# Giving VectorE's order by hand in the v stage, with 64 more gathered columns, and moving a product of the gates three groups later

## The chip, the cores and the metric

The kernel runs on one core of one Trainium2 chip. The metric is the device time of one execution, in microseconds. Before the change it is 2059.61 us, the median of three runs (2057.92 to 2060.23). The engines of the core are named as in the profile: PE is TensorE (matmuls), PEld its weight loads, DVE is VectorE, ACT is ScalarE, POOL is GpSimd, SP is SyncE, which only issues DMAs here.

## What is computed

One layer of a streaming encoder for 256 tokens of 2048 columns: a convolution branch and a state-space branch, attention over 256 memory rows, then a layer of product-key experts, and a last RMS norm. Only the experts matter for the change:

```
idx, g = the 128 chosen experts of a token (8 heads x 16) and their gates
u = jnp.take(u_tab, it, axis=0)
act = jax.nn.gelu(jnp.einsum("td,tkd->tk", xt, u))
v = jnp.take(v_tab, it, axis=0)
return jnp.einsum("tk,tkd->td", gt * act, v)
```

There are 16384 experts; both tables are 16384 x 2048 in float32.

## The kernel before, in words

The 256 tokens lie in two tiles of 128 (tt = 0 and 1). The layers ahead of the experts are done by about 790 us and are not touched. The experts are computed in three stages.

**The u stage with the dense part.** Of each u row the first 768 columns are multiplied densely: `dense()` (L960) loads all 128 blocks of 128 experts, transposes them on PE (L972) and multiplies them by all tokens (L978). The other 1280 columns are gathered: `Route.dot` (L925) issues one indirect DMA of POOL per slot (L928, five buffers) and one DVE instruction that multiplies and sums (L930). There are 256 dots, counted by `tick`. The loop at L1125 writes the order of DVE out by hand (`manual_schedule`, L1122): what is emitted first runs first on DVE. `Pace` (L1076) feeds the routing and the dense part between the dots at so many steps per dot.

**Settling.** At dot number `SETTLE_AT` (L1131) the rest of the dense part is emitted, and from then on `settle()` (L1086) is paced at 2.2 steps per dot. Settling picks from the dense scores those of the chosen experts: per group of four tokens `onehots` (L992: PE, then ACT Relu), `select` (L1010: PE), `pick` (L1023: a DVE product, L1026, then PE, L1028). When all 32 groups of a tile are picked, `finish` (L909) adds the gathered part, takes the Gelu curve (L915) and multiplies by the gates (L918, DVE), and transposes the result back. Then `left` and `build` (L1031, L1047) write the coefficients of four tokens, spread over all 16384 experts, into `W[tt]`. The one-hot `L` of `left` is made either by PE and ACT (L1043, L1044) or by a DVE comparison (L1039); `route.tt and g % 2` says which. Tile 0 is picked first; its builds run among the picks of tile 1. `settle` runs `routes[0].finish()` between the two, with four steps of its own. What is left of the builds follows after the last dot, at L1157 to L1163, where the order of DVE is again the planner's.

**The v stage.** The output is the chosen v rows times their coefficients. Of the 2048 columns `DC` = 1472 are done densely: for each block b of 128 experts the loop at L1202 makes float32r high and low parts of the weights (`wh`, `wl`, L1208 on ACT and L1209 on DVE) and of the loaded rows (`split`, L102: `vh` on ACT, L103; `vl` on DVE, L104), and 18 matmuls accumulate in PSUM: two tiles, three column chunks of 512, 512 and 448, three products each (L1218 to L1220). The other `GC` = 576 columns are gathered: `gathered()` (L1178) issues one indirect DMA per slot (L1183, six buffers) and one DVE multiply-add into `accg` (L1185), 256 in all, a little over two per block. SP loads `vr` (L1211) four buffers ahead. `vh`, `vl`, `wh` and `wl` have two buffers each. In this stage a planner that simulates the engines sets the order on every engine; it may bring an instruction forward when its inputs are there. After the loop DVE adds the residual (L1228), ACT squares (L1229, L1230), and each tile is normed and stored (L1231 to L1242).

## Time and profile before

| | |
|---|---|
| median of three runs | 2059.61 us |
| the profiled execution | 2058.54 us |
| its span, first to last instruction | 2056.8 us |
| mean granted clock of PE over the span | 0.982 |
| PE busy | 1960.9 us, 95% of the span |
| DVE busy | 1681.5 us, 82% |
| ACT busy | 999.4 us, 49% |
| POOL busy | 786.2 us, 38% |
| all DMA | 571.78 MB, mean 278 GB/s |

The times of the rows are microseconds from the start of the span. Busy times of PE are modelled ends of pipelined matmuls, so neighbouring matmuls overlap in the rows; the distance between two starts is what one costs in a stream. A number in square brackets at the end of a row is the idle time of the engine just before it, and what ended it.

### The profile page before, as it was taken

Reading aid. Unit: us, or ns where it says so; the run is one execution under the profiler, and the core shown is the slowest. Engines: PE = TensorE matmul, PEld = TensorE weight load, DVE = VectorE, ACT = ScalarE, POOL = GpSimd, SP = SyncE. Lnnn points to the kernel's source line nnn. Section 1 sums busy time; section 2 is a strip of 40 time slices with the busy share of each in tenths; the row PEclk is TensorE's granted clock in tenths of the full one; section 3 lists DMA queues with packets and bytes.
Section 4 is the critical chain, followed back from the end, with each engine's and each line's share of the span. In section 5 each row is a group of like instructions: output and inputs, shape, how many; then the busy total and the mean of one; then the engine's idle time right before and its main releaser. Section 6 shows DMA issues by size and latency. Waiting matters only on the chain.

```text
span 2056.8 us, 33321 instructions
## 1 busy us (share of the span) xinstructions
PE 1960.9 (95%) x12361; PEld 1682.5 (82%) x12379; DVE 1681.5 (82%) x2757; ACT 999.4 (49%) x1586; POOL 786.2 (38%) x589
## 2 busy tenths in 40 slices
PE   7899999998999999999999999989999999999996
PEld 7888886786899888888888878867678888888885
DVE  6699999895665557999976667888869899899998
ACT  5775765454644445333333323556554444444444
POOL 1011111000000004443446655453128777677775
PEclk9999999999999999999999999999999999999998
DMA  8888788857855567999999999988539999999996
GB/s 245 198 226 222 202 220 227 229 179 221 286 174 177 168 203 266 305 312 321 322 363 403 408 390 396 302 289 266 160 143 337 359 339 336 346 339 336 342 339 226
DMA packets 203108, 571.78 MB, mean 278 GB/s; under 512 B 31410, under 2 KB 39459, under 8 KB 202818
## 3 DMA queue, kind: packets, MB, share of 16 engines
q1 hardware_dynamic: 135810, 307.48, 44.4%
q0 software_dynamic: 67136, 262.18, 38.0%
q8 instruction: 97, 1.59, 0.3%
q14 instruction: 65, 0.53, 0.1%
HBM read 556.74 MB, written 12.85 MB: 277 GB/s over the span
## 4 chain that ended last, share of the span: by engine, by line
PE 56%; DVE 15%; issue 11%; DMA 8%; POOL 7%; ACT 1%; SPq 0%; POOLq 0%; DVEq 0%; ACTq 0%
PE acc L1220 8%; PE acc L1219 8%; PE acc L1218 8%; POOL u L928 7%; DVE u L930 5%; PE mm L216 4%; PE mm L215 4%; PE mm L214 4%; PE mm L206 3%; PE mm L207 3%; PE mm L205 3%; PE pw L1054 3%; DMA w_lo<-in_w_kv_mem 3%; PE y L1019 1%; DMA xc<-in_mem 1%
## 5 line engine op out<-in xcount | busy, mean ns | idle before, releaser
L1183 POOL DMA_INDIRECT v<-in_peer_v,vidx x256 | 394.1, 1539 | 180.9 <-DVE accg L1185 70.5
L930 DVE SCALAR_TENSOR_TENSOR u<-u,hnF 128x1280 f32<-128x1280 f32 x256 | 384.5, 1505 | 81.5 <-DMA u<-in_peer_u,uidx 79.5
L928 POOL DMA_INDIRECT u<-in_peer_u,uidx x256 | 300.3, 1173 | 324.3 <-DVE u L930 235.6
L978 PE MATMUL sy<-hnT,ut 128*128 128x256 f32 x1536 | 357.5, 385 | 13.4 <-ACT ut L974 12.4
L191 ACT CAST w_hi<-w_raw 128x1024 fp32r<-128x1024 f32 (+2 forms) x228 | 231.4, 1017 | 246.1 <-PE mm L207 116.0
L978 PEld LDWEIGHTS sy<-hnT,ut 128*128 128x128 f32 x1536 | 287.2, 193 | 54.7 <-ACT ut L974 16.3
L196 DVE TENSOR_TENSOR w_lo<-w_raw,w_hi 128x1024 fp32r<-128x1024 f32 (+2 forms) x192 | 227.4, 1186 | 112.9 <-ACT w_hi L191 110.7
L103 ACT CAST vh<-vr 128x1472 fp32r<-128x1472 f32 x128 | 183.1, 1431 | 251.5 <-PE acc L1219 167.9
L1219 PE MATMUL acc<-vh,wl 128*128 128x512 f32 (+1 forms) x768 | 295.4, 385 | 0.0
L1220 PE MATMUL acc<-vl,wh 128*128 128x512 f32 (+1 forms) x768 | 293.7, 385 | 0.2 <-DVE vl L104 0.2
L216 PE MATMUL mm<-aT_hi,w_lo 128*128 128x256 f32 x960 | 270.6, 289 | 17.9 <-DMA w_lo<-in_w_in 6.8
L1218 PE MATMUL acc<-vh,wh 128*128 128x512 f32 (+1 forms) x768 | 275.9, 384 | 2.4 <-ACT vh L103 2.4
L214 PE MATMUL mm<-aT_hi,w_hi 128*128 128x256 f32 x960 | 276.2, 290 | 0.3 <-ACT w_hi L191 0.3
L215 PE MATMUL mm<-aT_lo,w_hi 128*128 128x256 f32 x960 | 273.8, 287 | 0.0
L104 DVE TENSOR_TENSOR vl<-vr,vh 128x1472 fp32r<-128x1472 f32 x128 | 216.7, 1693 | 45.5 <-ACT vh L103 34.7
L1185 DVE SCALAR_TENSOR_TENSOR accg<-v,coef,accg 128x576 f32<-128x576 f32 x256 | 208.6, 815 | 4.1
L216 PEld LDWEIGHTS mm<-aT_hi,w_lo 128*128 128x128 f32 x960 | 181.9, 193 | 24.4 <-DMA w_lo<-in_w_in 8.0
L214 PEld LDWEIGHTS mm<-aT_hi,w_hi 128*128 128x128 f32 x960 | 185.0, 193 | 5.8 <-issue 3.7
L215 PEld LDWEIGHTS mm<-aT_lo,w_hi 128*128 128x128 f32 x960 | 185.4, 193 | 3.4 <-issue 2.0
L974 ACT COPY ut<-ut 128x768 f32<-128x768 f32 x128 | 100.4, 800 | 168.0 <-PE ut L972 143.8
L1219 PEld LDWEIGHTS acc<-vh,wl 128*128 128x128 f32 x768 | 144.5, 188 | 30.6 <-DVE wl L1209 0.4
L1218 PEld LDWEIGHTS acc<-vh,wh 128*128 128x128 f32 x768 | 144.7, 188 | 28.3 <-ACT vh L103 2.6
(385 smaller groups left out, 3233.3 us busy)
## 6 DMA issues: line engine op xcount, KB each, us to landing
vr<-in_peer_v SPq DMA_DIRECT2D x128, 736.0 KB
raw<-in_peer_u SPq DMA_DIRECT2D x127, 384.0 KB
w_raw<-in_w_kv_mem SPq DMA_DIRECT2D x64, 512.0 KB
w_raw<-in_w_in SPq DMA_DIRECT2D x48, 512.0 KB
w_raw<-in_w_out SPq DMA_DIRECT2D x32, 512.0 KB
w_raw<-in_w_q_mem SPq DMA_DIRECT2D x32, 512.0 KB
w_raw<-in_w_o_mem SPq DMA_DIRECT2D x32, 512.0 KB
w_lo<-in_w_kv_mem POOLq DMA_DIRECT2D x24, 512.0 KB
```

The source lines that it names most:

```text
L191: S.copy(hi, raw)
L196: V.tensor_sub(lo, raw, hi.bitcast(F32))
L214: PE.matmul(o, wh, ah, start=first and cb % 2 == 0, stop=False, skip_group_check=True)
L215: PE.matmul(o, wh, al, start=False, stop=False, skip_group_check=True)
L216: PE.matmul(o, wl, ah, start=False, stop=last and end, skip_group_check=True)
L928: G.indirect_dma_start(out=u, out_offset=None, in_=a["peer_u"].rearrange("e (q c) -> (e q) c", c=GU), in_offset=bass.IndirectOffsetOnAxis( ...
L930: V.scalar_tensor_tensor(u, u, 1.0, hnF[:, self.tt, :], op0=ALU.mult, op1=ALU.mult, accum_out=self.act[:, j:j + 1])
L978: PE.matmul(ps[:, b % 2, :], ut[:, k, :], hnT[:, k, :], start=k == 0 and b % 2 == 0, stop=k == KD - 1 and b % 2 == 1, skip_group_check=True)
L1183: G.indirect_dma_start(out=v, out_offset=None, in_=table, in_offset=bass.IndirectOffsetOnAxis(ap=vidx[tt][:, j:j + 1], axis=0))
L1218: PE.matmul(o, wh[:, tt, :], vh[:, cs_], start=b == 0, stop=False)
L1219: PE.matmul(o, wl[:, tt, :], vh[:, cs_], start=False, stop=False)
L1220: PE.matmul(o, wh[:, tt, :], vl[:, cs_], start=False, stop=b == NB - 1)
```

## The change

- `GC` goes from 576 to 640, so `DC` from 1472 to 1408 and the third column chunk from 448 to 384.
- In the v stage the order of DVE is given by the program. Weights are split for two blocks at once (`WGROUP` = 2, tiles of 128 x 256, three buffers), one group ahead, among the gathers of every odd block. Within a block and tile the products with `vl` come after all those with `vh`. The products of tile 1 in the last two blocks come after all others. Gathers are asked for at the same pace as before.
- A Sqrt on a scratch column is emitted at block 110.
- In `settle`, `routes[0].finish()` is begun where it was, and its second half (the product with the gates, the transpose back) is emitted at group 3 of tile 1.
- `left` of tile 1 uses DVE's comparison in 21 groups of 32 where it used it in 16.
- `SETTLE_AT` goes from 176 to 179.

```diff
-GC = 576
+GC = 640
-WL_POOL = 0
+WGROUP = 2
+EARLY = 8
-SETTLE_AT = 176
+SETTLE_AT = 179
...
+    eps_j = consts.tile([P, 1], F32, name="eps_j")
...
-        if route.tt and g % 2:
+        if route.tt and g % 3:
             V.tensor_tensor(L, bc(iota[:, None, :P], [P, 4, P]), bc(route.gT[:, 1, 4 * g:4 * g + 4, None], [P, 4, P]),
...
             for n in range(groups + lag):
+                if (tt, n) == (1, 3):
+                    run(finishing)
...
-                yield from routes[0].finish()
+                finishing = routes[0].finish()
+                next(finishing)
...
     gathering = gathered()
-    done = 0
+
+    def weights(b, tt):
+        wh, wl = (vs.tile([P, WGROUP, P], F32R, name=nm, bufs=3) for nm in ("wh", "wl"))
+        split(wh, wl, W[tt][:, b:b + WGROUP, :])
+        return wh, wl
+
+    def products(b, tt, wh, wl, vh, vl):
+        outs = [(acc[tt][:, c, :cs_.stop - cs_.start], cs_) for c, cs_ in enumerate(COLS)]
+        for o, cs_ in outs:
+            PE.matmul(o, wh, vh[:, cs_], start=b == 0, stop=False)
+            PE.matmul(o, wl, vh[:, cs_], start=False, stop=False)
+        for o, cs_ in outs:
+            PE.matmul(o, wh, vl[:, cs_], start=False, stop=b == NB - 1)
+
+    order.enter_context(tc.manual_schedule(engines={mybir.EngineType.DVE}))
+    late = []
+    ahead = [weights(0, tt) for tt in range(NTT)]
     for b in range(NB):
         if b == TAIL_AT:
             load_tail()
-        wh = vs.tile([P, NTT, P], F32R, name="wh")
-        wl = vs.tile([P, NTT, P], F32R, name="wl")
-        for tt in range(NTT):
-            S.copy(wh[:, tt, :], W[tt][:, b, :])
-            (G if tt < WL_POOL else V).tensor_sub(wl[:, tt, :], W[tt][:, b, :], wh[:, tt, :].bitcast(F32))
+            S.activation(eps_j, eps_t, AF.Sqrt)
+        i = b % WGROUP
+        if i == 0:
+            now, ahead = ahead, []
         vr = vraw_p.tile([P, DC], F32, name="vr")
         SY.dma_start(vr, a["peer_v"][b * P:(b + 1) * P, :DC])
         vh = vs.tile([P, DC], F32R, name="vh")
         vl = vs.tile([P, DC], F32R, name="vl")
         split(vh, vl, vr)
         for tt in range(NTT):
-            for c, cs_ in enumerate(COLS):
-                o = acc[tt][:, c, :cs_.stop - cs_.start]
-                PE.matmul(o, wh[:, tt, :], vh[:, cs_], start=b == 0, stop=False)
-                PE.matmul(o, wl[:, tt, :], vh[:, cs_], start=False, stop=False)
-                PE.matmul(o, wh[:, tt, :], vl[:, cs_], start=False, stop=b == NB - 1)
-        while done * NB < (b + 1) * (NTT * NSLOT + 8) and done < NTT * NSLOT:
-            next(gathering)
-            done += 1
+            x = b, tt, now[tt][0][:, i, :], now[tt][1][:, i, :], vh, vl
+            if tt and b >= NB - 2:
+                late.append(x)
+            else:
+                products(*x)
+        for n in range(b * (NTT * NSLOT + EARLY) // NB, (b + 1) * (NTT * NSLOT + EARLY) // NB):
+            next(gathering, None)
+            if i == WGROUP - 1 and b < NB - 1 and len(ahead) < NTT:
+                ahead.append(weights(b + 1, len(ahead)))
+    for x in late:
+        products(*x)
+    order.close()
```

## Rows read from the trace of the kernel before

**Rows 1.** Busy by stretch: PE, PEld, DVE, ACT, POOL; granted clock, DMA share, GB/s.

```profile
1200.00:1290.00 90.00, 81.97 (x422) 70.44 (x421) 61.52 (x82) 25.33 (x47) 53.68 (x40) 0.96 1.01 395
...
1376.00:1420.00 44.00, 42.81 (x504) 32.62 (x511) 41.13 (x62) 25.38 (x46) 17.35 (x19) 0.96 0.88 285
...
1700.00:1800.00 100.00, 100.00 (x453) 84.78 (x452) 89.72 (x126) 46.34 (x77) 71.18 (x49) 1.00 0.95 342
```

**Rows 2.** Timeline, one block of the v stage: start, length, engine, line, operation, idle before.

```profile
2027.78 1.43 ACT L103 CAST vh<-vr 128x1472 fp32r<-128x1472 f32 x1 [2.16 <-PE acc L1219]
...
2028.71 0.39 PE L1218 MATMUL acc<-vh,wh 128*128 128x512 f32 x1
...
2029.24 1.69 DVE L104 TENSOR_TENSOR vl<-vr,vh 128x1472 fp32r<-128x1472 f32 x1 [0.30 <-ACT vh L103]
...
2029.39 0.36 PE L1218 MATMUL acc<-vh,wh 128*128 128x448 f32 x1
...
2030.00 0.39 PE L1219 MATMUL acc<-vh,wl 128*128 128x512 f32 x1
...
2030.06 1.70 POOL L1183 DMA_INDIRECT v<-in_peer_v,vidx  x1 [0.30 <-issue]
...
2030.85 0.28 DVE L1209 TENSOR_TENSOR wl<-WA,wh 128x128 fp32r<-128x128 f32 x1
...
2031.26 1.67 DVE L1185 SCALAR_TENSOR_TENSOR accg<-v,coef,accg 128x576 f32<-128x576 f32 x2
...
2031.77 1.43 ACT L103 CAST vh<-vr 128x1472 fp32r<-128x1472 f32 x1 [2.16 <-PE acc L1219]
```

**Rows 3.** Groups of instructions, v stage: busy us, mean ns | idle before, releasers.

```profile
L1183 POOL DMA_INDIRECT v<-in_peer_v,vidx x256 | 394.1, 1539 | 180.9 <-DVE accg L1185 70.5 <-ACT WB L1055 60.4 <-issue 39.1
...
L104 DVE TENSOR_TENSOR vl<-vr,vh 128x1472 fp32r<-128x1472 f32 x128 | 216.7, 1693 | 45.5 <-ACT vh L103 34.7 <-issue 10.4
L1185 DVE SCALAR_TENSOR_TENSOR accg<-v,coef,accg 128x576 f32<-128x576 f32 x256 | 208.6, 815 | 4.1
```

**Rows 4.** Timeline, the waits of DVE and PE in settling.

```profile
1294.84 0.69 DVE L1026 TENSOR_TENSOR H<-H,y 128x512 f32<-128x512 f32 x1 [5.70 <-PE y L1016]
...
1361.19 0.29 DVE L918 TENSOR_TENSOR cT<-cT,gT 128x128 f32<-128x128 f32 x1 [5.54 <-ACT cT L915]
...
1366.46 0.65 PE L1028 MATMUL more<-H,onecol 128*32 128x128 f32 x8 [4.60 <-DVE H L1026]
```

**Rows 5.** The end: last matmul; group of gathered products after 2039.9; DVE's last product.

```profile
2039.54 0.36 PE L1220 MATMUL acc<-vl,wh 128*128 128x448 f32 x1
...
L1185 DVE SCALAR_TENSOR_TENSOR accg<-v,coef,accg 128x576 f32<-128x576 f32 x6 | 4.9, 813 | 0.0
...
2051.83 1.41 DVE L1240 SCALAR_TENSOR_TENSOR WB<-WB,rms_st,WA 128x512 f32<-128x512 f32 x2
```

**Rows 6.** Chain that ended last: twelve float32r matmuls of 256 columns in attention.

```profile
594.80 1.44 PE ss L704 x12
```

**Rows 7.** Groups of instructions: DVE operations of the same two kinds, other widths.

```profile
L930 DVE SCALAR_TENSOR_TENSOR u<-u,hnF 128x1280 f32<-128x1280 f32 x256 | 384.5, 1505 | 81.5 <-DMA u<-in_peer_u,uidx 79.5
...
L104 DVE TENSOR_TENSOR pT<-ppt,pT 128x256 fp32r<-128x256 f32 x8 | 3.0, 419 | 0.8 <-ACT pT L103 0.8
```

**Rows 8.** Sixteen matmuls of `select` after PE's wait and later; a stretch (columns as rows 1).

```profile
1367.04 1.98 PE L1019 MATMUL y<-E,WB 128*64 128x128 f32 x16
...
1370.37 1.09 PE L1019 MATMUL y<-E,WB 128*64 128x128 f32 x16
...
1366.00:1369.20 3.20, 2.74 (x27) 2.06 (x28) 3.20 (x6) 0.73 (x2) 2.59 (x3) 0.50 0.89 270
```

**Rows 9.** Timeline, POOL at the start of the v stage.

```profile
1525.60 0.95 POOL L1183 DMA_INDIRECT v<-in_peer_v,vidx  x1 [60.35 <-ACT WB L1055]
...
1532.02 0.95 POOL L1183 DMA_INDIRECT v<-in_peer_v,vidx  x1 [0.30 <-DMA v<-in_peer_v,vidx]
```

**Rows 10.** Groups of instructions: the matmul that makes a one-hot in `left`, tile 1.

```profile
L1043 PE MATMUL d<-C,hnT 128*128 128x512 bf16 x16 | 6.1, 378 | 1.4 <-ACT L L1044 1.4
```

## The prediction

> **What bounds the kernel now.** I read the busy times by stretch first. In the v stage PE is busy for all of 100 us at a granted clock of 1.00, DVE for 90, ACT for 46, POOL for 71; settling, too, is PE's for most of its length (42.8 of 44 us, DVE 41.1) [rows 1]. So I went on to one block of the v stage in the timeline. The conversions of `vh` of two neighbouring blocks start 3.99 us apart, which is the block's period; ACT stood idle for 2.16 us before each, until PE freed the buffer [rows 2]. The block's DVE work is `vl` to `wl` 1.61 us, two `wl` 0.41 us, two gathered products 1.67 us: 3.69 us, then an idle 0.30 us until ACT has the next `vh` [rows 2]. The groups show that `accg` never waited for its gather's data, while POOL waited for `accg` to free buffers [rows 3]. So PE sets the period; DVE is close behind, ACT and the loads are not. Last I looked for stretches where PE isn't the bound, and found two: a standstill in settling, in which DVE waits 5.54 us for the Gelu curve and PE then 4.60 us for DVE [rows 4], and the end, where DVE still has six gathered products to do after PE's last matmul [rows 5].
>
> The sum is made against the profiled execution, 2058.54 us (span 2056.8 and 1.7 around it), which is 1.07 us under the median of 2059.61.
>
> **v stage, fewer dense columns.** 768 matmuls (128 blocks, 2 tiles, 3 products) lose 64 columns. Three matmuls of 512 columns in a row start within 0.68 us (2028.71 to 2029.39), three of 448 within 0.61 us (2029.39 to 2030.00): 227 and 203 ns, or 23 ns for 64 columns [rows 2]. Twelve of 256 columns took 1.44 us, 120 ns each, so 448 to 256 gives 28 ns for 64 columns [rows 6]. The bounds are 768 x 23 = 18.0 and 768 x 28 = 21.3 us; I take 20.5, the figure at a full 2.4 GHz (64 columns in 26.7 ns), which lies between. A block becomes 3.99 - 0.16 = 3.83 us.
>
> **Who has to keep up.** DVE: `vl` shrinks by 64 x (1693 - 419)/(1472 - 256) = 67 ns [rows 3, 7] to a pitch of 1.54 us. Splitting weights for two blocks costs one 256-wide instruction of 419 ns per block in place of 0.41 us, between 0.33 us (with the overlap of 0.08 that the rows show) and 0.42. A gathered product grows by 64 x (1505 - 815)/(1280 - 576) = 63 ns [rows 3, 7] to 0.90 us, times 2.06 per block 1.85. Sum 3.72 to 3.81 us against PE's 3.83. DVE fits, without room. But now it runs in written order, so each wait stops all behind it. Three places:
>
> - The weights of tile 1 for the next two blocks are the fourth tile in a ring of three. They wait until PE has done tile 0 of the odd block (half a block, 1.9 us), then for a conversion of ACT, an estimate of 0.4 us (1.43 us for 1472 columns makes 0.25, and a fixed part). I place DVE's queue from there: `vl` of the next block starts 2.9 us after PE starts the odd block. It must be ready when PE gets to the `vl` products, now after six others, 1.3 us into its block, so it may start at 3.5. PE doesn't stop; cover left 0.5 us.
> - In one block of sixteen a third gathered product (0.90 us) stands ahead of that `vl`: cover exceeded by 0.3 to 0.4 us, seven times, +2.0 (0 to 3).
> - At the start, two gathered products stand ahead of the second block's `vl`. POOL issued the first gather at 1525.60, and its landing ended a wait at 1532.02 [rows 9]: 6.4 us. I take +2.0 (0 to 6.4; the larger end if nothing else hides the landing, none if the first gathers are issued earlier).
>
> SP's queue is not lengthened: `vr` is smaller and asked for as before. POOL issues as many gathers as before, each 2560 bytes a row in place of 2304. v stage together: -16.5 us, between -21 and -8.
>
> **Settling.** With the gates' product at group 3, DVE goes on with three or so dots and the first pick in place of the 5.54 us [rows 4]; by then the curve is long there. PE's 4.60 us hang on a pick of DVE that comes earlier by as much. After the standstill PE's sixteen matmuls of `select` took 1.98 us, later 1.09: the granted clock was 0.50 in this stretch, the lower level of 1.2 GHz, after PE had stood idle [rows 8]; 0.9 us that go too. -6.4 in all (0 if another wait takes its place, -7.5 at most). The curve's second half is needed first by `build` at group 5, so there are two groups of cover; the coefficients of tile 0, which the v stage alone reads, are not urgent. What is late next is PE itself: after the standstill it has no such wait.
>
> Starting at dot 179: DVE waited 5.70 us at the first pick for PE to get through the end of the dense part [rows 4]. Three dots of 1.5 us fit there. That shortens no PE work; it lightens DVE later, where PE is the bound. I take +0.3 (-2 to +1), the pick being a little later.
>
> Five fewer one-hots by PE: at most 5 x 0.38 = 1.9 us [rows 10]; DVE gets five products of 0.7 us in a stretch where it has gaps. -1.0 (0 to -1.9). Settling together: -7.1.
>
> **The end.** PE's last matmul starts at 2039.54 and ends at 2039.90; the span ends 16.9 us later. With DVE's order written out the gathered products come in time with the blocks and are asked for by block 124, so the six left over, 4.9 us, are gone. Tile 1's products of the last two blocks (about 3.8 us) come after all of tile 0, so tile 0's sums can lie beside PE. What DVE does for tile 0 last, three products of which two of 512 columns take 1.41 us as they do for tile 1 [rows 5], some 2.2 us in all, then goes from behind PE's end as well, in whole or in part: between 4.9 and 7.1 us. I take -6.3, the nearer to the upper end, as 3.8 us of PE are cover enough. The early Sqrt waits for nothing, so the planner may place it anywhere; if a table load stays in the end, tile 0's falls beside PE: 0.
>
> **Sum:** -16.5 - 7.1 - 6.3 = -29.9; 2058.54 - 29.9 = 2028.6, at the median 2029.7. I say **2030**.
>
> **Rivals.**
>
> *A: the loads become the bound of the v stage.* A block moves 128 x 1408 x 4 bytes of `vr` and 2.06 gathers of 128 x 640 x 4, 1.397 MB, where it was 1.362. At 3.83 us that is 365 GB/s. The DMA engines' share was 0.95 at 342 GB/s [rows 1], so by it they are full at 360: 3.88 us per block. The v stage then gains 128 x 0.11 = 14 less 4, and the whole comes to 2036. Against it: the stretch from 1200 to 1290 had 395 GB/s [rows 1], and no conversion in the block shown waited for a load [rows 2]. The Trainium skill (SBUF — State Buffer, Summary: rules for kernel authors) says to reckon with about 358 GB/s between HBM and SBUF; by it a block would take 3.90 us and the kernel 2039. The trace's 395 GB/s says otherwise.
>
> *B: the ring stops PE.* If ACT takes the weights' conversion ahead of the next block's `vh`, `vh` is done 1.4 us after it, at 3.9 us, and `vl` at 5.5 where PE wants it at about 5.0: 0.5 us in each of 64 odd blocks, +32, hence 2061. For it: ACT's order is the planner's. Against: `vh` is free half a block earlier than the weights.
>
> *C (slower): POOL can't issue fast enough.* A gather's issue takes 0.95 us alone [rows 9] and 1.70 when it falls into `vl` [rows 2]; mean 1.54 [rows 3]. With DVE nearly gapless every issue may fall so: 2.06 x (1.70 + 0.30) = 4.12 us per block, and DVE, in order, waits for the data and PE for DVE. The v stage loses 128 x 0.13 = 17 us and the 2 of the start; less 13.4 elsewhere, 2064. It decides from a mean issue of 1.63 us (3.99 / 2.06 - 0.30) on; below it the v stage still gains. Against it: six buffers in hand, and DVE's subtractions from SBUF take no larger part of a block than before. The Trainium skill (SBUF — State Buffer, Who interferes with whom) says that a two-input DVE operation contends only with GpSimd's reads and is inferred not to hold up descriptor generation; by it issues would stay at 0.95 and C would fall. The 1.70 us beside `vl` says that something holds them.
>
> *D: settling isn't mended.* The standstill returns as a wait of the first picks for PE, or of dots for gathers, as the group order is not the time order. Then 2030 + 7 = 2037.
>
> **How the numbers follow.** A measurement of this kernel tells 0.2%, some 4 us. Forecast 0.66, A 0.11, D 0.08, B 0.07, C 0.08. B lies within 4 us of before. Faster 0.85, same 0.07, slower 0.08. The range takes the forecast's bounds, from 2021 (v -20, settling -9.5, end -7) up, and A and D with the v stage at its weak end, to 2046.
>
> **What would show it.** In the v stage: starts of neighbouring `vh` conversions 3.83 us apart, the narrow matmuls at 0.175 us, PE busy throughout, DVE at 97%. DVE's wait at L918 gone, and PE's 4.60 us with it. After PE's last matmul no L1185 and 10 to 11 us to the end. Wrong if PE shows waits for `vl` in odd blocks (B), if `accg` waits for DMA (A or C: C if POOL has no gaps, A if the share is at 1.0), or if the standstill shows under another line (D).

## The result and the profile after

The changed kernel takes 2050.22 us (median of eight runs, 2045.56 to 2053.99); the kernel before, on the same chip, 2060.89. The ratio is 0.9941 [0.9927, 0.9955]: 0.6% faster, where 1.4% was forecast, and outside the range that was given. The two profiled executions differ by 12 us: 2046.4 against 2058.54.

I cut both traces at three events of the timeline: the start of the last dense matmul, the start of the first v product (`acc`), and the end of the last one. From the first to the second is settling, from the second to the third the v stage. The lengths are differences of rounded times, good to 0.1 us.

| us | before | after | change | forecast |
|---|---|---|---|---|
| up to the last dense matmul | 1291.8 | 1293.9 | +2.1 | 0 |
| settling | 235.4 | 222.2 | -13.2 | -7.1 |
| v stage | 512.7 | 513.9 | +1.2 | -16.5 |
| the end | 16.9 | 14.6 | -2.3 | -6.3 |
| span | 2056.8 | 2044.6 | -12.2 | -29.9 |

The first line is code that nobody touched; over all profiled executions of this study it lies between 1291.6 and 1304.4 us. So single executions are compared by their stages.

**v stage.** The narrow chunk's matmuls now start 0.175 us apart (0.203 before), as forecast. Adding up by how much a matmul starts later than its predecessor's stream distance gives PE's stops: 1.8 us before, 21.4 after. Without them the stage went from 510.9 to 492.5 us. So the column saving came, 18.4 us, and PE's stops ate it: 14.7 us of them stand at the step from a `vh` product to the first `vl` product (L1219), and 5.7 more at the product right behind such a stop, which starts 0.10 us late each time.

The stretch that answers to the last of [rows 1], with the same columns:

```profile
1700.00:1800.00 100.00, 99.05 (x455) 82.72 (x455) 90.94 (x104) 43.76 (x54) 76.91 (x53) 1.00 0.98 363
```

The granted clock is 1.00 as before, DVE hardly busier (90.9 for 89.7), and PE no longer full. The groups of the changed kernel's page that answer to [rows 3] (busy us, mean ns | idle before, releasers):

```profile
L1189 POOL DMA_INDIRECT v<-in_peer_v,vidx x256 | 360.2, 1407 | 191.9 <-DVE accg L1191 80.6
...
L1191 DVE SCALAR_TENSOR_TENSOR accg<-v,coef,accg 128x640 f32<-128x640 f32 x256 | 225.1, 880 | 5.7 <-DMA v<-in_peer_v,vidx 3.6
L105 DVE TENSOR_TENSOR vl<-vr,vh 128x1408 fp32r<-128x1408 f32 x128 | 208.5, 1630 | 0.0
...
L1219 PE MATMUL acc<-vl,wh 128*128 128x512 f32 (+1 forms) x768 | 190.6, 383 | 6.0 <-DVE vl L105 5.1
```

POOL's issues are no longer than before, gathered data is not late, and `vl` itself waits for nothing. What DVE waits for stands ahead of `vl`, in the waits of the changed kernel:

```profile
DVE wl L105 <- ACT wh L104: 44.5, 53, 3.3
...
DVE wl L105 <- ACT vh L104: 7.8, 10, 0.8
```

All but 3.1 us of these are waits for tile 1's next weights, the fourth tile in a ring of three (`wl<-WB`): in 62 of the 63 odd blocks that split weights, 0.79 us on average. One odd block in the timeline, to be held against [rows 2] (start, length, engine, line, operation):

```profile
1697.85 0.40 PE L1216 MATMUL acc<-vh,wh 128*128 128x512 f32 x1
...
1700.23 0.34 PE L1217 MATMUL acc<-vh,wl 128*128 128x384 f32 x1
...
1700.40 1.44 PE L1219 MATMUL acc<-vl,wh 128*128 128x512 f32 x6
1700.65 1.38 ACT L104 CAST vh<-vr 128x1408 fp32r<-128x1408 f32 x1 [2.69 <-PE acc L1217]
...
1701.93 0.40 ACT L104 CAST wh<-WB 128x256 fp32r<-128x256 f32 x1
...
1702.36 0.43 DVE L105 TENSOR_TENSOR wl<-WB,wh 128x256 fp32r<-128x256 f32 x1 [0.77 <-ACT vh L104]
...
1702.70 1.67 DVE L105 TENSOR_TENSOR vl<-vr,vh 128x1408 fp32r<-128x1408 f32 x1
...
1704.06 0.34 PE L1217 MATMUL acc<-vh,wl 128*128 128x384 f32 x1
...
1704.42 0.75 PEld L1219 LDWEIGHTS acc<-vl,wh 128*128 128x128 f32 x4 [0.35 <-DVE vl L105]
```

Two orders are to be seen that the program does not write. PE does the twelve `vh` products of both tiles first (1697.85 to 1700.40) and then the six `vl` products, in every block but the last; the program has tile 0 whole, then tile 1. And ACT, freed by the twelfth `vh` product, converts the `vh` of two blocks on first, 1.38 us, and only then the weights for which DVE stands. From there: `wl`, `vl`, and PE, which is ready 0.2 us before. PE's last `vh` product of the odd block starts at 1700.23 and the `vl` products that hang on it at 1704.42, 4.19 us later; PE's own work between the two is 4.0.

**Settling.** The answer to [rows 4], DVE's and PE's rows of the timeline:

```profile
1293.49 1.49 DVE L933 SCALAR_TENSOR_TENSOR u<-u,hnF 128x1280 f32<-128x1280 f32 x1 [1.16 <-DMA u<-in_peer_u,uidx]
...
1296.95 0.69 DVE L1029 TENSOR_TENSOR H<-H,y 128x512 f32<-128x512 f32 x1
...
1363.61 0.29 DVE L921 TENSOR_TENSOR cT<-cT,gT 128x128 f32<-128x128 f32 x1 [0.92 <-ACT cT L918]
```
```profile
1369.99 0.43 PE L1031 MATMUL more<-H,onecol 128*32 128x128 f32 x8 [0.74 <-DVE H L1029]
```

The first pick (L1029) no longer waits 5.70 us, since dots fill the hole; the wait at the curve fell from 5.54 to 0.92 us and PE's 4.60 to 0.74.

**The end.** The answer to [rows 5]:

```profile
2029.39 1.75 DVE L1253 TENSOR_TENSOR WA<-WA,acc 128x512 f32<-128x512 f32 x3 [3.32 <-PE acc L1219]
2031.06 1.74 DVE L1253 TENSOR_TENSOR WB<-WB,acc 128x512 f32<-128x512 f32 x3
```
```profile
2.04 0.20 ACT L1227 ACTIVATE eps_j<-eps_t 128x1 f32<-128x1 f32 x1
...
2034.42 1.28 ACT L113 ACT_TABLE_LOAD   x1
```

No gathered product is left behind PE's end (2030.0). But tile 0's sums (`WA`) stand there, not beside PE: DVE waited 3.32 us for tile 0's last `vl` product, which in PE's order comes late. The early Sqrt did not spare the load of a table in the end: the planner had it done at 2.04 us of the execution, long before the Gelu curve of settling, for which another table was loaded at 1362.01.

### The profile page after: what moved, and what is told of

Its sections match the earlier page's. It is cut to its first block, busy times and chain, and to the rows that moved or that the text cites. A ratio compares the mean times of both kernels' runs of the same rounds, so it can differ in the third digit from the quotient of the medians.

```text
span 2044.6 us, 33063 instructions
## 1 busy us (share of the span) xinstructions
PE 1950.3 (95%) x12357; PEld 1667.9 (82%) x12374; DVE 1674.5 (82%) x2634; ACT 979.4 (48%) x1455; POOL 739.7 (36%) x589
## 4 chain that ended last, share of the span: by engine, by line
PE 62%; DVE 17%; DMA 10%; issue 5%; ACT 4%; POOL 1%; SPq 0%; DVEq 0%; ACTq 0%; POOLq 0%
PE acc L1219 7%; PE sy L981 7%; PE acc L1217 7%; PE acc L1216 7%; DVE u L933 5%; PE mm L219 4%; PE mm L218 4%; PE mm L217 4%; PE mm L209 3%; PE mm L210 3%; PE mm L208 3%; PE pw L1057 3%; DMA w_lo<-in_w_kv_mem 3%; PE d L1002 2%; PE y L1022 2%
## 5 line engine op out<-in xcount | busy, mean ns | idle before, releaser
L1189 POOL DMA_INDIRECT v<-in_peer_v,vidx x256 | 360.2, 1407 | 191.9 <-DVE accg L1191 80.6
L931 POOL DMA_INDIRECT u<-in_peer_u,uidx x256 | 287.7, 1124 | 325.2 <-DVE u L933 239.6
L981 PE MATMUL sy<-hnT,ut 128*128 128x256 f32 x1536 | 357.7, 385 | 13.8 <-ACT ut L977 11.8
L981 PEld LDWEIGHTS sy<-hnT,ut 128*128 128x128 f32 x1536 | 287.6, 193 | 55.5 <-ACT ut L977 14.6
L199 DVE TENSOR_TENSOR w_lo<-w_raw,w_hi 128x1024 fp32r<-128x1024 f32 (+2 forms) x192 | 227.6, 1187 | 112.6 <-ACT w_hi L194 112.2
L104 ACT CAST vh<-vr 128x1408 fp32r<-128x1408 f32 x128 | 176.0, 1375 | 265.7 <-PE acc L1217 223.1
L1216 PE MATMUL acc<-vh,wh 128*128 128x512 f32 (+1 forms) x768 | 287.6, 376 | 2.8 <-ACT vh L104 2.8
L1217 PE MATMUL acc<-vh,wl 128*128 128x512 f32 (+1 forms) x768 | 287.6, 376 | 0.0
L1191 DVE SCALAR_TENSOR_TENSOR accg<-v,coef,accg 128x640 f32<-128x640 f32 x256 | 225.1, 880 | 5.7 <-DMA v<-in_peer_v,vidx 3.6
L105 DVE TENSOR_TENSOR vl<-vr,vh 128x1408 fp32r<-128x1408 f32 x128 | 208.5, 1630 | 0.0
L1219 PE MATMUL acc<-vl,wh 128*128 128x512 f32 (+1 forms) x768 | 190.6, 383 | 6.0 <-DVE vl L105 5.1
L1219 PEld LDWEIGHTS acc<-vl,wh 128*128 128x128 f32 x768 | 137.4, 188 | 40.6 <-DVE vl L105 23.0
```

What stands on the lines that cost most here:

```text
L199: V.tensor_sub(lo, raw, hi.bitcast(F32))
L931: G.indirect_dma_start(out=u, out_offset=None, in_=a["peer_u"].rearrange("e (q c) -> (e q) c", c=GU), in_offset=bass.IndirectOffsetOnAxis( ...
L981: PE.matmul(ps[:, b % 2, :], ut[:, k, :], hnT[:, k, :], start=k == 0 and b % 2 == 0, stop=k == KD - 1 and b % 2 == 1, skip_group_check=True)
L1189: G.indirect_dma_start(out=v, out_offset=None, in_=table, in_offset=bass.IndirectOffsetOnAxis(ap=vidx[tt][:, j:j + 1], axis=0))
L1216: PE.matmul(o, wh, vh[:, cs_], start=b == 0, stop=False)
L1217: PE.matmul(o, wl, vh[:, cs_], start=False, stop=False)
```

## The experiments

Stages of the profiled execution of every run, as above. "Stops" are PE's in the v stage. A ratio with its interval is that of timed runs to the kernel before.

| run | settling | v stage | stops | end | ratio |
|---|---|---|---|---|---|
| before | 235.4 | 512.7 | 1.8 | 16.9 | 1 |
| after | 222.2 | 513.9 | 21.4 | 14.6 | 0.9941 [0.9927, 0.9955] |
| ring4 | 222.1 | 518.4 | 25.9 | 14.4 | 0.9934 [0.9912, 0.9956] |
| rows3 | 221.8 | 506.6 | 14.1 | 14.6 | 0.9902 [0.9881, 0.9923] |
| pe_written | 221.9 | 500.9 | 8.4 | 10.6 | 0.9844 [0.9823, 0.9864] |
| settle_auto640 | 222.2 | 495.8 | 6.4 | 56.9 | 1.0044 [1.0027, 1.0061] |
| ring4_vg5 | 222.1 | 529.2 | 36.8 | 14.4 | 1.0015 [0.9996, 1.0033] |
| ring4_pe_written | 224.9 | 529.9 | 37.5 | 10.6 | one run, 2064.68 us |
| fourth_late | 227.6 | 513.2 | 20.8 | 14.6 | 0.9930 [0.9905, 0.9956] |
| thin_products | 221.8 | 512.5 | 20.1 | 14.6 | 0.9932 [0.9911, 0.9953] |
| half_rows | 221.8 | 515.7 | 23.3 | 14.7 | one run, 2052.77 us |
| late_half_rows | 221.7 | 513.8 | 22.9 | 14.6 | one run, 2052.94 us |
| late_pe_written | 222.5 | 510.4 | 18.0 | 10.6 | 0.9889 [0.9872, 0.9905] |
| late_pe_rows3 | 221.8 | 508.1 | 15.6 | 10.5 | 0.9910 [0.9889, 0.9931] |
| stt_pe_written | 224.4 | 498.7 | 6.2 | 10.5 | 0.9840 [0.9814, 0.9866] |

### PE's order

```diff
-    order.enter_context(tc.manual_schedule(engines={mybir.EngineType.DVE}))
+    order.enter_context(tc.manual_schedule(engines={mybir.EngineType.DVE, mybir.EngineType.PE}))
```

> The changed kernel with PE's order, too, given by the program in the v stage: tile 0's products with vl before tile 1's products with vh, and tile 1's last two blocks behind everything. Theory 1: tile 0's weights come free half a block earlier, DVE's wait for tile 1's weights falls under 20 us; vl is wanted half a block earlier in its turn, so the gain is smaller than the ring's, 5 to 15 us under the changed kernel, and the end behind PE's last matmul shrinks from 14.6 to about 11 us. Theory 2: DVE has no time for that, PE waits for vl in every block: 5 to 20 us slower than the changed kernel. Theory 3: no change but for the end.

The v stage took 500.9 us and the end 10.6; 2031.1 us in all. PE's and ACT's rows of an odd block, then DVE's:

```profile
1702.36 0.40 PE L1216 MATMUL acc<-vh,wh 128*128 128x512 f32 x1
...
1703.65 0.80 PE L1219 MATMUL acc<-vl,wh 128*128 128x512 f32 x3
...
1707.47 0.39 PE L1219 MATMUL acc<-vl,wh 128*128 128x512 f32 x1
```
```profile
1704.49 0.41 ACT L104 CAST wh<-WB 128x256 fp32r<-128x256 f32 x1 [1.15 <-PE acc L1219]
```
```profile
1704.92 0.43 DVE L105 TENSOR_TENSOR wl<-WB,wh 128x256 fp32r<-128x256 f32 x1 [0.54 <-ACT wh L104]
1705.27 1.62 DVE L105 TENSOR_TENSOR vl<-vr,vh 128x1408 fp32r<-128x1408 f32 x1
```

Here the odd block starts at 1702.36; tile 0 is done with its weights half a block later, ACT stands ready for them, and `vl` starts 2.91 us after the block. PE comes to the `vl` products at 1707.47, 0.6 us after it ends. With the order of PE that the prediction assumed, its figures for this step hold. DVE's wait for tile 1's weights fell from 49 to 35 us only, not under 20 as Theory 1 had it; but what is left of it no longer stops PE.

The opposite, the planner's order on all engines with the 640 columns and the edits of settling:

```diff
-GC = 576
+GC = 640
...
-SETTLE_AT = 176
+SETTLE_AT = 179
...
-        if route.tt and g % 2:
+        if route.tt and g % 3:
...
+                if (tt, n) == (1, 3):
+                    run(finishing)
...
-                yield from routes[0].finish()
+                finishing = routes[0].finish()
+                next(finishing)
```

> The changes in settling together with 640 gathered columns, but the v stage's loop and its planner-made order as before the change. Theories 1 and 2: without the written order nothing stands behind a wait; the v stage takes its 20 us, the block 3.83 us, and the whole lies 15 to 20 us under the changed kernel, ratio 0.983 to 0.987. Theory 3: the block stays at 3.95 us or more, ratio 0.992 to 0.996.

The columns' gain is all there (495.8 us), and more than given back in the end. DVE's largest group behind PE's last matmul:

```profile
L1188 DVE SCALAR_TENSOR_TENSOR accg<-v,coef,accg 128x640 f32<-128x640 f32 x31 | 27.4, 884 | 16.7 <-DMA v<-in_peer_v,vidx 16.6
```

Thirty-one gathered products were put off. What the written order of DVE buys is that these come in time.

### What makes `vl` late

```diff
-        wh, wl = (vs.tile([P, WGROUP, P], F32R, name=nm, bufs=3) for nm in ("wh", "wl"))
+        wh, wl = (vs.tile([P, WGROUP, P], F32R, name=nm, bufs=4) for nm in ("wh", "wl"))
...
-VR_BUFS = 4
+VR_BUFS = 3
```

The run ring4 has both edits, rows3 the second alone.

> The changed kernel with a ring of four buffers for the split weights in place of three; to make room the loaded rows have three buffers in place of four. Theory 1 (the ring): DVE's wait for tile 1's weights (49 us over the v stage of the changed kernel) falls under 15 us, the products with vl no longer find PE waiting, and the time falls 12 to 18 us under the changed kernel's, ratio to before 0.985 to 0.989. Theory 2 (DVE is simply full in written order): no change, ratio 0.993 to 0.996; DVE's wait moves to vl. Theory 3 (the loads are the bound): no gain or slower, with more conversions that wait for the loaded rows (15.6 us in the changed kernel).

> The changed kernel with three buffers for the loaded rows in place of four, and nothing else: the other half of the run beside it. Theories 1 and 2: as the changed kernel, ratio to before 0.993 to 0.996. Theory 3: slower than the changed kernel by 5 us or more, as the loads have less room.

With four tiles the wait for the weights fell from 49.4 to 1.1 us, and PE's stops grew from 21.4 to 25.9. The fourth tile was paid for with a buffer of the loads, and in the waits of this run ACT now waits for loads, and DVE for gathered data:

```profile
ACT vh L104 <- DMA vr<-in_peer_v: 129.9, 66, 5.0
...
DVE accg L1191 <- DMA v<-in_peer_v,vidx: 49.6, 43, 2.9
```

Taking the buffer alone (rows3) made the v stage 7 us shorter. An odd block's first `vh` product and ACT's rows show how:

```profile
1701.26 0.40 PE L1216 MATMUL acc<-vh,wh 128*128 128x512 f32 x1
...
1701.59 1.38 ACT L104 CAST vh<-vr 128x1408 fp32r<-128x1408 f32 x1 [1.73 <-DMA vr<-in_peer_v]
...
1704.67 0.41 ACT L104 CAST wh<-WB 128x256 fp32r<-128x256 f32 x1 [1.70 <-PE acc L1219]
```

The conversion of `vh` now comes with its load, 1.70 us before PE frees the weights, and no longer stands between PE and them. So I tried the fourth tile against a gather buffer, with PE's order as the planner has it and as written:

```diff
-VG_BUFS = 6
+VG_BUFS = 5
...
-        wh, wl = (vs.tile([P, WGROUP, P], F32R, name=nm, bufs=3) for nm in ("wh", "wl"))
+        wh, wl = (vs.tile([P, WGROUP, P], F32R, name=nm, bufs=4) for nm in ("wh", "wl"))
```

> The changed kernel with four tiles in place of three in each ring of weights, paid for with one of the six buffers of gathered rows, so that the four buffers of the loads stay (the earlier run with four weight tiles had given one of these up). PE's order stays the planner's. Ring theory (the fourth tile, waiting for PE to end the odd block, makes vl late): DVE's wait for the weights, 49.4 us, falls under 5, PE's stops of 21.4 us to 8 or less, v stage about 500 us, ratio 0.988. Rival (the ring is only where the lateness shows; with PE's order by the planner DVE, in written order, is late by another wait): v stage 510 us or more. If five gather buffers are too few, accg shows waits for DMA of over 20 us.

> Four weight tiles and five gather buffers, with PE's order in the v stage as written too. With three tiles PE's stops were 8.4 us and the v stage 500.9. If the fourth tile's wait is what is left of the stops: v stage 493 to 496 us, ratio about 0.981. If it is covered by then, as the prediction worked out for this order (0.5 us of cover): 499 to 502, ratio 0.984 to 0.986; more than that and the sixth gather buffer was worth something.

Neither was faster than the kernel before. DVE waits for gathered data longer than in ring4, which had six buffers (49.6 us), so five are probably too few; no run has five gather buffers and nothing else:

```profile
DVE accg L1191 <- DMA v<-in_peer_v,vidx: 60.7, 48, 2.9
```

Next, the same ring, with tile 1's next weights behind the next block's `vl` in DVE's order, so that no buffer is given up:

```diff
         split(vh, vl, vr)
+        if len(now) < NTT:
+            now.append(weights(b, 1))
...
-            if i == WGROUP - 1 and b < NB - 1 and len(ahead) < NTT:
+            if i == WGROUP - 1 and b < NB - 1 and len(ahead) < NTT - 1:
```

> The changed kernel with one thing moved in DVE's written order: tile 1's weights of the next two blocks stand behind the next block's vl in place of ahead of it. Rings, buffers and PE's order (the planner's) as in the changed kernel. Ring theory (the fourth weights, waiting for PE to end the odd block, make vl late): DVE's wait of 49.4 us for these weights falls under 10, PE's stops before vl products fall from 20.3 to 8 us or less, v stage 513.9 to about 500, ratio 0.987 or 0.988. Rival 1 (vl is late anyway, as gathered data or DVE's own pace make it): v stage 510 or more. Rival 2 (the later weights are now late themselves): PE's stops move to the products with tile 1's weights, v stage 510 or more, with the stop at that line.

The wait for the weights is gone, the time is not. DVE's waits and POOL's group (1550 to 2000 us):

```profile
DVE accg L1191 <- DMA v<-in_peer_v,vidx: 44.1, 42, 2.4
DVE wl L105 <- ACT wh L104: 7.8, 7, 3.1
```
```profile
L1189 POOL DMA_INDIRECT v<-in_peer_v,vidx x235 | 377.7, 1607 | 76.4 <-issue 34.6 <-DVE accg L1191 20.9 <-DVE wl L105 15.9
```

POOL needs (377.7 + 76.4) / 235 = 1.93 us for a gather, 235 x 0.30 us of the 76.4 being the pause between two issues that every row has. 2.06 gathers a block make 3.98 us: that is about the block's period here (513.2 / 128 = 4.01). Three theories were left: DVE's own pace, the loads, and the loop PE, ACT, DVE, PE in the changed kernel with POOL's issuing behind it. They are told apart by taking away DVE's work, or the bytes:

```diff
-                V.scalar_tensor_tensor(accg[tt], v, coef[tt][:, j:j + 1], accg[tt], op0=ALU.mult, op1=ALU.add)
+                w = GU if j % 4 == 3 else GC
+                V.scalar_tensor_tensor(accg[tt][:, :w], v[:, :w], coef[tt][:, j:j + 1], accg[tt][:, :w], op0=ALU.mult, op1=ALU.add)
```

> The changed kernel with every fourth gathered product made on 64 of its 640 columns (the other 576 of that row are left out of the sum, so this leaves computation out); every gather is still issued and lands, every order and buffer is the changed kernel's. Theory, DVE's pace: in written order DVE's period is its work plus what it must wait, 3.61 us busy and 0.39 of waiting for the fourth weights make the 4.00 us measured per block, over PE's 3.83. 64 products less by some 0.75 us take 0.38 off DVE's work per block: PE's stops fall from 21.4 us to 5 or less, v stage from 513.9 to 497 or less, ratio 0.985. Rival, loads and the gathers' round trip (v stage 507 or more, as the moved weights and the fourth tile gave only a new wait for gathered data): PE's stops stay over 14 us and DVE's waits for data grow.

My theory of DVE's pace fell. The stage kept its length, and the work taken away came back as waiting for the same weights (44.5 and 7.8 us before):

```profile
DVE wl L105 <- ACT wh L104: 86.7, 64, 3.9
```

```diff
-                G.indirect_dma_start(out=v, out_offset=None, in_=table,
+                G.indirect_dma_start(out=v[:, :GC // 2], out_offset=None, in_=table,
...
+                both = accg[tt].rearrange("p (a c) -> p a c", a=2)
+                V.scalar_tensor_tensor(both, bc(v[:, None, :GC // 2], [P, 2, GC // 2]), coef[tt][:, j:j + 1], both, op0=ALU.mult, op1=ALU.add)
```

> The changed kernel with each gather fetching the first 320 of its 640 columns, and the product made on these 320 twice over (so the other half of the gathered columns is left out of the result). Gathers, their indices, DVE's 640 columns a product, orders and buffers are unchanged; a block moves 1.06 MB in place of 1.40. Loop theory (PE frees vh after the block's twelve vh products; ACT then converts the vh of two blocks on, 1.38 us, and only behind it the fourth weights, 0.40 us; DVE makes their wl, 0.43, and vl, 1.62, for which PE waits): bytes play no part, the v stage stays within 3 us of 513.9 and DVE's wait for the fourth weights within 10 us of 49.4. Loads theory (rival A of the prediction): v stage under 505.

> The same halved gathers in the kernel with the fourth weights behind the next block's vl (v stage 513.2, DVE's wait for the weights gone, 44 us of waits for gathered data in its place). There POOL was taken for 235 gathers by 377.7 us of issuing at 1.61 us each and 76.4 us between them, 1.93 us a gather; 2.06 gathers a block make 3.99 us, the period measured. POOL theory (rival C of the prediction, now as what comes after the loop): half the bytes change nothing in issuing, v stage 508 or more, POOL without gaps over 0.30 us. Loads theory: gathers land earlier, the 44 us fall under 15 and the v stage under 502.

Bytes play no part in either. The same 100 us of half_rows, then of late_half_rows (PE, PEld, DVE, ACT, POOL; clock, DMA share, GB/s):

```profile
1640.00:1740.00 100.00, 98.30 (x449) 81.35 (x448) 89.57 (x103) 42.16 (x51) 74.10 (x52) 1.00 0.79 264
```
```profile
1640.00:1740.00 100.00, 95.37 (x441) 79.98 (x440) 88.09 (x100) 41.58 (x49) 84.34 (x52) 1.00 0.76 258
```

The DMA engines have a fifth of their time free, and the v stage stands at 515.7 and 513.8 us, each a single execution. In the first POOL has time to spare, and DVE waits 53.5 us for the weights: the loop. In the second POOL is taken, 52 issues of 1.62 us and 52 pauses of 0.30 fill the 100 us:

```profile
L1189 POOL DMA_INDIRECT v<-in_peer_v,vidx x232 | 379.9, 1637 | 71.7 <-issue 27.2 <-DVE accg L1192 25.0 <-DVE wl L105 16.2
```

### Is there more with PE's order written?

The later weights, and these with three load buffers, on top of pe_written (edits as above):

> The changed kernel with PE's order as written (2031.1 us, v stage 500.9 with the DVE order of the change) and tile 1's next weights behind the next block's vl. DVE's account for PE as written was 3.60 us busy and 0.27 idle, nearly all of it the wait for these weights (35.9 us), 3.87 in all. If that wait goes and nothing replaces it: PE's 3.83, v stage 495 or 496, ratio 0.982. If the wait for gathered data replaces it, as it did with PE's order by the planner: 500 or more, ratio 0.985 or more. The loads' share was 1.00 at 364 to 373 GB/s, which makes 3.75 to 3.84 us for a block's 1.397 MB, so under 493 isn't expected of any theory.

> As the kernel with PE as written and the later fourth weights, with three buffers for the loads of v rows in place of four. With PE's order by the planner the third buffer less took 7 us off the v stage (513.9 to 506.6). If fewer loads standing in the DMA queues let the gathers land earlier: v stage no longer than with four, issue to landing of a gather shorter, ratio 0.982 or less. If the loads are then late themselves: conversions wait for loads by over 100 us and the v stage is 3 us or more longer than with four.

The wait for the weights fell from 38.1 us to 4.2, and 38.2 us of waiting for gathered data came; both are slower than pe_written. In pe_written POOL already has no time left (374.3 + 76.1 us for 240 gathers, 1.88 us each, 3.87 us a block), and the loads have none either:

```profile
1640.00:1740.00 100.00, 99.81 (x467) 85.35 (x467) 93.49 (x107) 45.03 (x52) 83.48 (x55) 1.00 0.99 364
```
```profile
L1189 POOL DMA_INDIRECT v<-in_peer_v,vidx x240 | 374.3, 1560 | 76.1 <-DVE wl L105 31.3 <-issue 24.1 <-DVE accg L1191 20.4
```

Neither is late there yet: DVE waited for gathered data twice, at the start of the stage (4.0 us), and no conversion waited for a load after 1618 us.

Last, whether POOL's issues get shorter when DVE makes `vl` and `wl` by another operation (in a copy of `split` that the v stage alone uses):

```diff
-        V.tensor_sub(lo, src, hi.bitcast(F32))
+        V.scalar_tensor_tensor(lo, src, 1.0, hi.bitcast(F32), op0=ALU.mult, op1=ALU.subtract)
```

> The kernel with PE's order as written (2031.1 us, v stage 500.9; POOL's issuing 1.56 us mean and 0.31 between makes 3.87 us a block, its period), with vl and wl made by DVE as a scalar_tensor_tensor of the same values (src times 1 less hi) in place of a tensor subtraction. If it is the plain subtraction that holds up POOL's issuing (an issue beside vl took 1.70 us and one between DVE's work 0.95): mean issue under 1.3 us, period 3.83 or less, v stage 493 to 496, ratio 0.981. If any work of DVE on two inputs holds it: mean issue 1.5 to 1.6, v stage 500 to 502, ratio 0.984. If the other form is slower on DVE (gathered products of that form took 0.88 us for 640 columns): v stage longer than 503.

They don't; mean 1.552 us against 1.560:

```profile
L1193 POOL DMA_INDIRECT v<-in_peer_v,vidx x240 | 372.6, 1552 | 75.0 <-DVE wl L109 31.0 <-issue 24.1 <-DVE accg L1195 18.7
```

Its 2030.33 us can't be told from the 2031.1 of pe_written. These two are the fastest kernels of the study.

### The parts of settling

All on the kernel before, with its own v stage.

```diff
+                if (tt, n) == (1, 3):
+                    run(finishing)
...
-                yield from routes[0].finish()
+                finishing = routes[0].finish()
+                next(finishing)
```

> The kernel before with the second half of the gates' finish asked for three groups later, and nothing else. From the last dense matmul to the first v product the kernel before took 235.4 us, the changed kernel 222.2. Theory 1 (the prediction's: the standstill at the Gelu curve is what settling gains): 228 to 229 us here, DVE's 5.54 us wait and PE's 4.60 us gone, ratio about 0.997. Theory 2 (the finish gives all of the 13 us): 222 us, ratio 0.9935. Theory 3 (the standstill only moves unless the three dots of the other edit are there too): over 232 us.

```diff
-SETTLE_AT = 176
+SETTLE_AT = 179
```

> The kernel before with settling begun at dot 179 in place of 176, and nothing else. Theory 1 (the prediction's: three dots fill DVE's 5.70 us wait for the end of the dense part, but DVE isn't what bounds settling): 235 to 236 us from the last dense matmul to the first v product, ratio 1.000. Rival (DVE bounds settling too, so three dots of 1.5 us done in a hole are worth their whole length): 230 to 231 us, ratio 0.9975.

```diff
-        if route.tt and g % 2:
+        if route.tt and g % 3:
```

> The kernel before with one one-hot in three, in place of one in two, left on PE (five made by DVE), and nothing else. Prediction's figure: 1.0 us (0 to 1.9) off 235.4, so 234.4. Rival (if the finish and the dot add up without more): 5 to 6 us, so 229 to 230; DVE's waits for PE at that line and the next, 6.0 and 3.3 us, fall to half.

The first two together, and then all three:

> The later finish and the start at dot 179 together, with one one-hot in two on PE as before. Sum theory (the parts add up, and the one-hots give the rest): 3.1 + 4.0 off 235.4, so 228 us from the last dense matmul to the first v product. Rival (the two need each other: with DVE's dots done in the first hole, the standstill's end comes wholly to PE; the one-hots give the 1.0 that the prediction had): 223 us.

> The kernel before with the three edits of settling (later finish, dot 179, one one-hot in three on PE) and its own v stage. From the last dense matmul to the first v product: before 235.4 us, changed 222.2; the finish alone gave 3.1 of it and the start at 179 alone 4.0. If the edits of settling stand by themselves: 222 us, the v stage at 512 to 513 us and the end at 17 us as before, ratio 0.9935. If part comes from the v stage's written order, whose first tiles and loads lie in settling: 225 us or more.

| run | settling | of it up to the last dot | ratio |
|---|---|---|---|
| before | 235.4 | 182.7 | 1 |
| finish_alone | 232.3 | 177.9 | 0.9999 [0.9981, 1.0017] |
| at179_alone | 231.4 | 174.9 | 1.0009 [0.9989, 1.0029] |
| onehots_alone | 231.3 | 180.2 | one run, 2061.43 us |
| finish_at179 | 223.2 | 170.0 | one run, 2048.22 us |
| settling_alone | 222.2 | 170.0 | 0.9957 [0.9938, 0.9976] |

The three edits give their 13.2 us whatever the v stage is: settling lies between 221.7 and 222.5 in twelve of the fifteen profiled executions that have them, and at 224.4 to 227.6 in three. The timed runs of settling_alone say 8.9 us (5 to 13). The parts don't add up: 3.1 and 4.0 alone, 12.2 together; and neither moves the timed runs alone by more than these can tell. The five one-hots give 1.0 us on top of the other two, as forecast, though 4.1 alone. DVE's rows of finish_alone, and of at179_alone:

```profile
1296.44 0.69 DVE L1026 TENSOR_TENSOR H<-H,y 128x512 f32<-128x512 f32 x1 [7.25 <-PE y L1016]
...
1362.97 0.29 DVE L918 TENSOR_TENSOR cT<-cT,gT 128x128 f32<-128x128 f32 x1 [0.89 <-ACT cT L915]
```
```profile
1294.65 0.69 DVE L1026 TENSOR_TENSOR H<-H,y 128x512 f32<-128x512 f32 x1 [2.77 <-PE y L1016]
...
1360.96 0.29 DVE L918 TENSOR_TENSOR cT<-cT,gT 128x128 f32<-128x128 f32 x1 [5.50 <-ACT cT L915]
```

Each closes its own hole and leaves the other's open. Part of what both together give beyond the sum is TensorE's clock. The stretches of settling at the lower of its two levels (a granted 0.50, 1.2 GHz), before, then in finish_alone and at179_alone, and the whole of settling in finish_at179 (columns as above):

```profile
1363.50:1370.30 6.80, 3.61 (x36) 2.35 (x36) 6.80 (x11) 1.19 (x2) 5.58 (x5) 0.50 0.62 176
1377.20:1380.60 3.40, 3.34 (x21) 2.80 (x19) 3.40 (x5) 0.87 (x3) 1.48 (x2) 0.50 0.90 286
```
```profile
1474.20:1481.00 6.80, 6.09 (x24) 5.01 (x25) 2.27 (x4) 1.67 (x3) 0.00 (x0) 0.50 0.36 112
```
```profile
1364.20:1371.00 6.80, 4.54 (x44) 3.20 (x46) 6.80 (x11) 1.79 (x3) 5.58 (x5) 0.50 0.74 242
```
```profile
1293.40:1516.60 223.20, 214.42 (x2409) 167.62 (x2424) 195.94 (x296) 139.27 (x253) 69.31 (x71) 1.00 0.69 226
```

Before, the first of these came while PE stood idle for 4.60 us [rows 4]; in finish_alone, PE had been busy for 3.2 of the 6.2 us ahead of it. If half of PE's busy time in such a stretch is what the level costs (an estimate), it is 3.5 us before, 3.0 and 2.3 with one edit, and nothing with both. That is 1.8 of the 5.1 us that the sum lacks. The rest isn't settled: the single figures are of one execution each, and an execution can be some 5 us long, as the three above.

## Why the prediction was wrong

**The step that failed** is the place of the weights: "They wait until PE has done tile 0 of the odd block (half a block, 1.9 us), then for a conversion of ACT ... `vl` of the next block starts 2.9 us after PE starts the odd block. It must be ready when PE gets to the `vl` products, now after six others, 1.3 us into its block, so it may start at 3.5." Both halves read PE's order off the program, although only DVE's order is written there and PE's is the planner's. In the trace `vl` starts 4.85 us after the odd block (1697.85 to 1702.70), for two reasons. Tile 0's `vl` products, and with them its weights, are done only after all twelve `vh` products: in rows3, where ACT stands ready, the weights' conversion starts 3.41 us after the block (1701.26 to 1704.67), in pe_written 2.13. And here ACT takes the `vh` of two blocks on first, which makes it 4.08. `vl` has more time, too, as PE comes to it after twelve others: 1704.24 less 1.6 is 4.8 us after the block. The cover of 0.5 us became a small lack: 34 stops of 0.15 to 0.23 us in 64 odd blocks, and smaller ones. With the 0.10 us behind each they make some 13 us. pe_written shows the step right under its own assumption: 2.91 us measured for 2.9, and a cover of 0.6 for 0.5. That its whole time is near the forecast, 2031.1 us for 2030, is luck in part: its v stage gained 11.8 us for 16.5, its settling 13.5 for 7.1.

**Right in size.** The columns: 18.4 us, in the bounds of 18.0 to 21.3 (the lower one is 17.7 by the factors as printed). The third gather in one block of sixteen: with PE's order written, seven stops of 0.26 us 61.8 us apart, 1.8 us for the 2.0 forecast (0 to 3).

**Larger in the changed kernel.** Five of the third gathers stop PE there for 0.94 us and two for 0.23 and 0.26, 5.2 us in all. At the start, for which 2.0 was taken, the first `vl` product that had to wait came 1.15 us late; with PE's order written it was 2.72. The lower end of the range is 2022 by its own terms, not 2021.

**The end** was out for the same reason: tile 0's last product came at PE's end. With PE's order written the end took 10.6 us, 6.3 less than before, which is the figure forecast. The table load stayed, as allowed for.

**Settling** was under-sized, 7.1 for 13.2. The step is "That shortens no PE work; it lightens DVE later, where PE is the bound. I take +0.3": the dots in the hole were worth about 4 us alone and 9.1 on top of the finish (3.0 of these the clock's, by the estimate above). That DVE, busy for 41.1 of 44 us there [rows 1], is why is likely, not shown. The clock was under-sized as well, 0.9 us for the 3.5 estimated above.

**The rivals.** B had the place right, the odd block's weights and ACT's order, but the order reversed: not the weights ahead of `vh`, but `vh` ahead of the weights. A (the loads) is excluded in the changed kernel by half_rows; with PE's order written the share did reach 0.99 to 1.00, at 364 to 373 GB/s, where the estimate had put the limit at 360. The Trainium skill (SBUF — State Buffer, Summary: rules for kernel authors) has about 358 GB/s there; these stretches exceed it. C (POOL) is not what happened, but it is what comes next: wherever the loop was cut or shortened with six gather buffers kept, POOL had next to no free time beyond the pauses (2 to 13 of 450 us), at mean issues of 1.55 to 1.64 us. C had put the point at which nothing is gained at 1.63, and fourth_late and late_half_rows, with 1.61 and 1.64, gained nothing. The Trainium skill's inference that a `tensor_tensor` of DVE does not hold up descriptor generation (SBUF — State Buffer, Who interferes with whom) does not carry over to these issues: all means lie over the 0.95 us that an issue takes alone [rows 9], and the last section shows what they end with. D (settling not mended) fell.

## What to carry to other kernels

When one engine's order is written by hand and the others' is left to a planner, the other engines' orders are unknown until they are read from a trace; a cover worked out from the program's text holds only for an order that is enforced. Where a queue is in written order, cutting one wait is worth only the distance to the next limit, so find that one first: here ring, POOL's issuing and the loads lay within 5% of each other. Taking work away from the suspect (DVE's products, the bytes) settled in three runs what moving waits about had left open in four.

## What the hardware showed that I had not expected

The mean issue of a run lay between 1.39 us (thin_products, least DVE work) and 1.64, and single ones in many runs took 3.5; in the kernel before the longest was 3.16. The rows tell what sets this. Of the 5120 issues of v rows in the twenty traces, 994 took 0.94 to 1.00 us. Every one of the other 4126 ended 0.81 to 0.84 us after the end of a DVE instruction: in 3915 cases the one that was under way when the issue began, in 211 a later one, with DVE running on without a pause. In the changed kernel, DVE's product ends at 1701.59 and the issue at 1702.41:

```profile
1700.71 0.88 DVE L1191 SCALAR_TENSOR_TENSOR accg<-v,coef,accg 128x640 f32<-128x640 f32 x1
...
1700.79 1.62 POOL L1189 DMA_INDIRECT v<-in_peer_v,vidx  x1 [0.30 <-DVE wl L105]
```

In fourth_late, an issue that lasts over the ends of two DVE instructions; the third, `wl`, ends at 1715.14 and the issue at 1715.96:

```profile
1712.47 3.49 POOL L1189 DMA_INDIRECT v<-in_peer_v,vidx  x1 [0.30 <-DVE wl L105]
...
1714.72 0.42 DVE L105 TENSOR_TENSOR wl<-WB,wh 128x256 fp32r<-128x256 f32 x1
```

It is so behind the subtractions (`vl`, `wl`) and behind the multiply-adds (`accg`) alike, which fits stt_pe_written: another form of the operation changed nothing. So the fewer pauses DVE makes, the longer POOL is taken by an issue. That DVE's instruction is what holds the issue is read from these times; no run has changed it alone.
